# Who issues the stores of tiles that ScalarE makes last: SP or ScalarE

## The chip, the core and the metric

One core of a Trainium2 chip runs one program, the kernel. Its engines are TensorE (PE, with its weight loads as PEld), VectorE (DVE), ScalarE (ACT), GpSimd (POOL) and SyncE (SP). Each works through a queue of its own in order; they meet through semaphores. The metric is the device time of one execution in microseconds (us). In the profile, SPq and ACTq are the instruction queues of SP and ACT, in which DMAs are issued.

## The reference

One layer of a hybrid encoder, in float32, over 2048 tokens of width 1024:

```python
xn = rms_norm(x, mix_norm_g)
proj = xn @ w_in                  # aq ak av mq mk mv mo, two gate inputs, ga gm
att = chunk_band_attention(aq, ak, av, rel_bias)      # own chunk of 64 and 8 before
mqk = silu(causal_depthwise_conv(concat([mq, mk])))
hm = rms_norm(mlstm_chunkwise(mq_c, mk_c, mv, ipre + b_igate, fpre + b_fgate))
mlstm_out = sigmoid(mo) * hm
y = sigmoid(ga) * (att @ w_att_proj) + sigmoid(gm) * (mlstm_out @ w_mlstm_proj)
x = x + y @ w_out
hn = rms_norm(x, ffn_norm_g)
x = x + square(relu(hn @ w_up)) @ w_down              # hidden width 4096
out = rms_norm(x, final_norm_g)
```

## The kernel before

**Products.** A float32 product is made of three matmuls of fp32r parts (`mm3`, lines 644 to 646: a large and a small part on either side). The large weight matrices go through `quad` (line 727): a 2 by 2 block of weight tiles and of inputs is multiplied with seven products in place of eight, on sums and differences of the tiles; `quad_tok` (line 755) is the same for token tiles. A weight tile is loaded into `wraw` (lines 560, 565), split by ACT's cast (line 583) and DVE's difference (line 585) into the parts `wsp`, and sums of tiles are formed by DVE (line 602). PE takes `wsp` and the input parts `r`; the results come out of PSUM (`bank`) by ACT's copy (line 1859) and DVE's addition (line 1867) into `ctx` tiles.

**Stages.** The sequence is cut into two halves of two blocks each. In the trace, in us: up to 100 the norm and the first projections; 100 to 530 attention and recurrence of blocks 0 and 1, interleaved with projections; 530 to 700 the gates ga and gm of these blocks; 700 to 1100 the output product and the input products of blocks 2 and 3; 1100 to 1520 the up product of the first half; 1520 to 2070 its down product beside attention and recurrence of blocks 2 and 3; 2070 to 2250 the rest of that half's mixing; 2250 to 2500 the up product of the second half; then its down product and the final norm.

**Stores.** Tiles that don't fit into SBUF go to DRAM and are loaded again: kept projections `proj` (`keep_proj`, made by the copy of line 923), rows of norm scales (`row_out`, line 1125), values `mvfar` of the recurrence (`evac_mv`), gates `gate` and `mfar` (the finish of the gate and mo quads, lines 2000 and 2006), and the seven parts of the input to the down product, `u` (`keep` and `sums`; relu and square at lines 2198 and 2202, or sums on DVE). Every one of these goes through `store` (line 2120), which SP issues. All 2254 DMAs of the program are issued by SP.

**Order.** The program is written by generators; `Flow` runs them with priorities, pools of tiles and a clock for each engine. A yield such as `yield "sp", 900, 2000` tells it the engine, how long it is occupied and how much later the result is there. Then `Order` sorts the instructions of each engine anew by a list schedule: `cost` gives durations, `transfer`, `REACH` and `LAND` the time of a DMA over one shared queue, `due` the latest time, back from PE's sequence, `lag` the time of a signal, `MARGIN` the reserve behind an operation of another engine. The result is fixed as dependencies from each instruction to the next on its engine. The semaphores on which transfers report their landing aren't in this model: eight of them (DMAHW0 to DMAHW7 in the rows below) are given out in turn over the transfers of the program.

Of the kernel before, what the change touches and what calls it, by code (L numbers as in the profile page):

```python
# [30 lines left out]
P = 128  # L31
# [4 lines left out]
NT = T // P  # L36
# [33 lines left out]
class Event:  # L70
    def __init__(self):
        self.at = None
# [23 lines left out]
class Flow:  # L96
# [7 lines left out]
               act=dict(pe=220.0, act=130.0, dve=130.0, pool=180.0),  # L104
               dve=dict(pe=220.0, act=130.0, dve=130.0, pool=155.0), pool=dict(pe=290.0, act=130.0, dve=60.0),
               sp=dict())
# [106 lines left out]
def act_ns(n, ps=False, ap=0):  # L213
    return (51 if ps else 93) + 0.834 * n + 93 * ap
# [10 lines left out]
class Order:  # L225
# [6 lines left out]
    def __init__(self, tc):  # L232
        self.tc = tc
        name = lambda i: str(i.engine).split(".")[-1]
        self.ins = [i for i in tc.nc.cur_bb.bb.instructions if name(i) in self.WAKE and (i.ins or i.outs)]
        self.eng = [name(i) for i in self.ins]
        self.dur = [self.cost(i, e) for i, e in zip(self.ins, self.eng)]
        self.graph()

    @staticmethod  # L240
# [71 lines left out]

    def lag(self, j, k):
        e, to = self.eng[j], self.eng[k]
        if e == to != "SP":
            return 0.0
        t = self.WAKE[to] + (0.0 if e == "SP" else 13.0)
        return t + (0.0 if e != "PE" else 175.0 if self.dur[j] >= 140.0 else 130.0)

    def due(self):  # L320
        n, t = len(self.ins), 0.0
        due = [None] * n
        for k in range(n):
            if self.eng[k] == "PE":
                due[k] = t
                t += self.dur[k]
        for k in range(n - 1, -1, -1):
            d = t + 8000.0 if due[k] is None else due[k]
            less = self.dur[k] + (self.FAR if self.eng[k] == "SP" else 0.0)
            for j in self.succ[k]:  # L330
                d = min(d, due[j] - less - self.lag(k, j))
            due[k] = d
        return due

    def run(self):
        due, n = self.due(), len(self.ins)
        at, safe, left = [0.0] * n, [0.0] * n, self.left
        clock = dict.fromkeys(self.WAKE, 0.0)
        soon = {e: [] for e in self.WAKE}
        ripe = {e: [] for e in self.WAKE}  # L340
        order = {e: [] for e in self.WAKE}
        queue = 0.0
        for k in range(n):
            if not left[k]:
                heapq.heappush(soon[self.eng[k]], (0.0, due[k], k))
        for _ in range(n):
            t, e = min((clock[e] if ripe[e] else max(clock[e], soon[e][0][0]), e)
                       for e in self.WAKE if ripe[e] or soon[e])
            while soon[e] and soon[e][0][0] <= t:
                k = heapq.heappop(soon[e])[2]  # L350
                heapq.heappush(ripe[e], (k if e == "PE" else due[k], k))
            k = heapq.heappop(ripe[e])[1]
            order[e].append(self.ins[k])
            start = max(clock[e], at[k])
            clock[e] = end = start + self.dur[k]
            if e == "SP":
                queue = max(queue, start + self.REACH) + self.transfer(self.ins[k])
                end = queue + self.LAND
            for j in self.succ[k]:
                to = self.eng[j]  # L360
                r = end + self.lag(k, j)
                at[j] = max(at[j], r)
                safe[j] = max(safe[j], r + (self.MARGIN[e] if to != "PE" and (to != e or e == "SP") else 0.0))
                left[j] -= 1
                if not left[j]:
                    heapq.heappush(soon[to], (safe[j], due[j], j))
        for o in order.values():
            for a, b in zip(o, o[1:]):
                self.tc.add_manual_dep(b, a.name, mybir.DependencyInfo(
                    mybir.DependencyClass.NoSync, mybir.DependencyReason.DATA), reason="order")  # L370


class Layer:
# [215 lines left out]
    def quad_w(self, i, q, kept, raws, evs):  # L589
# [10 lines left out]
        def sub(n, dst, x, y):  # L600
            yield "dve", dve_ns(1024)
            V.tensor_sub(dst, x, y)  # L602
            if kept:
                fl.spawn(keep(n, dst), 1)
            else:
                fl.set(spilt[n])
# [312 lines left out]
    def keep_proj(self, x, j, bk):  # L919
        fl = self.fl  # L920
        (t,) = yield "get", self.temp, 1
        yield "act", act_ns(512, True)
        self.nc.scalar.copy(t[:, :512], bk)
        fl.put_dense(self.banks, bk)
        yield from self.store(self.projd.ap()[x, j], t[:, :512], self.proj_ev[x][j], self.temp, t)

    def merge_kept(self, j, t):

# [188 lines left out]
    def row_out(self, name, src):  # L1117

        fl, nc = self.fl, self.nc
        (t,) = yield "get", self.temp, 1  # L1120
        (bk,) = yield "get", self.banks, 1
        yield "pe", 220
        nc.tensor.transpose(bk[:NT, :P], src, self.ident)
        yield "act", act_ns(P, True)
        nc.scalar.copy(t[:NT, :P], bk[:NT, :P])
        fl.put(self.banks, bk)
        yield "sp", 900, 2000
        nc.sync.dma_start(self.rowd[name].ap().rearrange("(t p) -> t p", p=P), t[:NT, :P])
        fl.put(self.temp, t)

    def row_in(self, name, dst):
# [493 lines left out]
    def evac_mv(self, b, t, bk):  # L1625
        fl, nc = self.fl, self.nc
        (x,) = yield "get", self.ctx, 1
        yield "act", act_ns(512, True, 1 if b == 0 else 0)
        if b == 0:
            nc.scalar.mul(x[:, :512], bk, self.rr["x"][:, t:t + 1])  # L1630
        else:
            nc.scalar.copy(x[:, :512], bk)
        fl.put_dense(self.banks, bk)
        yield from self.store(self.mvfar[b].ap()[t], x[:, :512], self.mv_ev[b][t], self.ctx, x)

    def evac_conv(self, b, g, bk):
        fl = self.fl
# [263 lines left out]

    def keep(self, tiles, evs, k, dst, out):

        return self.sums(tiles, evs, lambda m, x: self.store(dst[m, k], x, out[m][k]), [e[k] for e in out])

    def sums(self, tiles, evs, go, sent):
        fl, V = self.fl, self.nc.vector
# [77 lines left out]
    def after_in(self, name, s):  # L1985
        fl, nc = self.fl, self.nc

        def finish(n, which, t, ps):
            hi, h = WHERE[which]
            b, j = 2 * s + h, 2 * hi + n  # L1990
            t5 = t[:, :512]
            if name in ("q", "k"):
                to, ev = (self.qfar, self.q_ev) if name == "q" else (self.kfar, self.k_ev)
                yield from self.parts(t, ps, 0.125 if name == "q" else 1.0, to[b].ap()[j], ev[b, j])
                return
            if name in ("mq", "mk"):
                yield from self.conv_far(b, (MH if name == "mk" else 0) + j, t, ps)
                return
            yield "act", act_ns(512)
            nc.scalar.activation(t5, t5 if ps is None else ps, AF.Tanh, scale=0.5)  # L2000
            if ps is not None:
                fl.put(self.banks, ps)
            if name == "mo":
                yield "act", act_ns(512, False, 2)
                g = self.ghead[:, j:j + 1]
                nc.scalar.activation(t5, t5, AF.Identity, scale=g, bias=g)
                dst, ev = self.mfar[b].ap()[2 * MH + j], self.m_ev[b, 2 * MH + j]
            else:
                x, j = name[:2] == "gm", 4 * hi + 2 * int(name[2]) + n
                if x and b == 0:  # L2010
                    yield from self.merge_kept(j, t)
                    return
                dst, ev = self.gd[b].ap()[int(x), j], self.g_ev[int(x), b, j]
            fl.spawn(self.store(dst, t5, ev, self.ctx, t), 1)

        return self.combine(finish, 3 if name in ("mq", "mk") else 0)

    def conv_far(self, b, g, z, ps):
# [99 lines left out]
    def store(self, dst, src, ev, pool=None, item=None):  # L2118
        yield "sp", 900, 2000
        self.nc.sync.dma_start(dst, src)  # L2120
        self.fl.set(ev)
        if pool is not None:
            self.fl.put(pool, item)
# [463 lines left out]
```

## Time and profile before

| | |
|---|---|
| median of 3 runs | 2779.6 us (2778.0 to 2780.48) |
| profiled execution | 2778.32 us, its span 2776.5 us |
| granted TensorE clock | 0.998 |
| busy: PE, DVE, ACT, POOL | 2751.0, 2057.1, 1494.5, 53.7 us |
| instructions: PE, DVE, ACT, POOL | 12994, 3783, 2608, 100 |
| DMA | 678.64 MB, 244 GB/s in the mean |

Busy time is the time in which an engine executes something; issuing a DMA does not count. A row of waits names the engine and line that stood still, the operation that ended its wait, and the total, the number and the longest of these waits in us. A row of a timeline gives start and duration in us, and in brackets the idle time before and what ended it. A row of DMA issues ends with the median us from issue to landing.

### The profile page before, as it was taken

How to read it: one execution, taken by the hardware profiler on the slowest of the kernel's cores; microseconds unless marked ns; L12 is line 12 of the kernel's file. 1: busy time of each engine (PE TensorE's matmuls, PEld its weight loads, DVE VectorE, ACT ScalarE, POOL GpSimd, SP SyncE). 2: the span in 40 equal slices, each digit the busy share in tenths (PEclk: the TensorE clock that was granted, in tenths of full speed). 3: DMA queues.
4: the chain of work that ended last, by engine and by line, in shares of the span. 5: the costliest groups of instructions: out<-in, count | busy, mean ns of one | idle time of the engine just before them, and what ended most of it. 6: DMA issues, size and time to landing. Idle time of an engine off the chain costs nothing.

```text
span 2776.5 us, 38600 instructions
## 1 busy us (share of the span) xinstructions
PE 2751.0 (99%) x12994; PEld 2286.5 (82%) x12994; DVE 2057.1 (74%) x3783; ACT 1494.5 (54%) x2608; POOL 53.7 (2%) x100
## 2 busy tenths in 40 slices
PE   9999999999999999999999999999999999999998
PEld 7888888888778878888888888888888888888887
DVE  7796789768996866886676688789888656556565
ACT  5564576535453535575555556565436655554443
POOL 0010001000000000000000000000000000000000
PEclk9999999999999999999999999999999999999999
DMA  7958759769755667579877887788777567666564
GB/s 273 291 195 276 230 166 304 250 222 319 262 199 204 220 243 256 198 270 325 288 280 273 287 245 233 230 256 253 251 261 261 206 220 261 243 238 217 189 230 149
DMA packets 329046, 678.64 MB, mean 244 GB/s; under 512 B 36840, under 2 KB 67728, under 8 KB 328848
## 3 DMA queue, kind: packets, MB, share of 16 engines
q1 hardware_dynamic: 328848, 676.18, 72.3%
q8 instruction: 102, 1.67, 0.2%
q14 instruction: 96, 0.79, 0.1%
HBM read 472.59 MB, written 203.44 MB: 243 GB/s over the span
## 4 chain that ended last, share of the span: by engine, by line
PE 91%; DMA 3%; DVE 3%; issue 2%; ACT 1%; SPq 0%; POOLq 0%; POOL 0%; DVEq 0%; ACTq 0%
PE bank L727 43%; PE bank L644 12%; PE bank L645 12%; PE bank L646 12%; PE bank L1415 2%; PE bank L1388 2%; PE bank L1446 2%; PE bank L755 2%; DVE wsp L585 1%; PE bank L1700 1%; PE bank L1701 1%; PE bank L1702 0%; PE bank L1686 0%; DMA wsum<-ctx 0%; ACT wsp L583 0%
## 5 line engine op out<-in xcount | busy, mean ns | idle before, releaser
L727 PE MATMUL bank<-r,wsp 128*128 128x512 f32 x5544 | 1265.5, 390 | 1.4 <-DVE ctx L1867 0.6
L727 PEld LDWEIGHTS bank<-r,wsp 128*128 128x128 f32 x5544 | 1038.0, 188 | 222.5 <-DVE ctx L1867 3.8
L585 DVE TENSOR_TENSOR wsp<-wraw,wsp 128x1024 fp32r<-128x1024 f32 x459 | 561.6, 1224 | 360.9 <-ACT wsp L583 335.2
L583 ACT CAST wsp<-wraw 128x1024 fp32r<-128x1024 f32 x459 | 482.5, 1052 | 464.1 <-PE bank L727 209.0
L644 PE MATMUL bank<-r,wsp 128*128 128x512 f32 x1472 | 586.1, 398 | 2.3 <-ACT r L1224 2.1
L645 PE MATMUL bank<-r,wsp 128*128 128x512 f32 x1472 | 574.8, 391 | 0.2 <-DVE r L1229 0.2
L646 PE MATMUL bank<-r,wsp 128*128 128x512 f32 x1472 | 574.9, 391 | 0.0
L646 PEld LDWEIGHTS bank<-r,wsp 128*128 128x128 f32 x1472 | 276.3, 188 | 58.7
L644 PEld LDWEIGHTS bank<-r,wsp 128*128 128x128 f32 x1472 | 276.9, 188 | 54.0 <-ACT r L1224 2.3
L645 PEld LDWEIGHTS bank<-r,wsp 128*128 128x128 f32 x1472 | 277.0, 188 | 50.5 <-DVE r L1229 0.5
L1867 DVE TENSOR_TENSOR ctx<-bank,ctx 128x512 f32<-128x512 f32 x186 | 127.1, 688 | 89.4 <-PE bank L727 89.2
L1229 DVE TENSOR_TENSOR r<-r 128x512 fp32r<-128x512 f32 x248 | 163.9, 687 | 25.3 <-ACT r L1224 24.5
L1224 ACT CAST r<-r 128x512 fp32r<-128x512 f32 x248 | 147.8, 624 | 49.8 <-DMA r<-u 47.0
L1859 ACT COPY ctx<-bank 128x512 f32<-128x512 f32 x186 | 107.9, 581 | 64.5 <-PE bank L727 60.9
L1430 ACT ACTIVATE sc<-sc,scs 128x640 f32<-128x640 f32 (+4 forms) x128 | 97.5, 763 | 71.7 <-DVE scs L1427 65.6
L2198 ACT ACTIVATE ctx<-ctx 128x512 f32<-128x512 f32 x96 | 60.6, 631 | 102.6 <-DVE ctx L1867 102.6
L1451 DVE TENSOR_TENSOR r<-bank,r 128x512 fp32r<-128x512 f32 (+1 forms) x168 | 97.1, 597 | 16.5 <-ACT r L1449 15.7
L1449 ACT CAST r<-bank 128x512 fp32r<-128x512 f32 (+1 forms) x168 | 81.8, 518 | 47.9 <-PE bank L1446 46.0
L1421 DVE CUSTOM_DVE_ANT_0 sc<-bank,bias 128x320 f32<-128x320 f32 (+3 forms) x240 | 103.7, 463 | 3.6 <-PE bank L1415 2.6
L1388 PE MATMUL bank<-r,r 128*128 128x512 f32 x336 | 96.0, 367 | 2.8 <-DVE r L1451 2.6
L602 DVE TENSOR_TENSOR wraw<-wraw,wraw 128x1024 f32<-128x1024 f32 x76 | 92.9, 1223 | 2.0
L552 DVE TENSOR_TENSOR ctx<-ctx,ctx 128x512 f32<-128x512 f32 x112 | 76.5, 688 | 17.7 <-DMA ctx<-in_wf 11.7
(258 smaller groups left out, 2720.7 us busy)
## 6 DMA issues: line engine op xcount, KB each, us to landing
wraw<-in_wf SPq DMA_DIRECT2D x178, 512.0 KB, 4.0
wraw<-wsum SPq DMA_DIRECT2D x136, 512.0 KB, 4.1
r<-u SPq DMA_DIRECT2D x224, 256.0 KB, 4.3
wraw<-in_w SPq DMA_DIRECT2D x88, 512.0 KB, 5.0
u<-ctx SPq DMA_DIRECT2D x128, 256.0 KB, 2.6
ctx<-in_wf SPq DMA_DIRECT2D x112, 256.0 KB, 4.3
wsum<-ctx SPq DMA_DIRECT2D x112, 256.0 KB, 3.6
u<-tmp SPq DMA_DIRECT2D x96, 256.0 KB, 3.7
```

The costliest lines, as they stand in the source:

```text
L583: nc.scalar.copy(w[:, 0], raw)
L585: nc.vector.tensor_sub(w[:, 1], raw, w[:, 0].bitcast(F32))
L644: mm(ps, lh, rh, start=first, stop=False)
L645: mm(ps, lh, rl, start=False, stop=False)
L646: mm(ps, ll, rh, start=False, stop=last)
L727: mm(ps, wv[:, x, k, n], a[:, y], start=new and k == 0 and x == y == 0, stop=k == 3 and x == 1, skip_group_check=True)
L1224: self.nc.scalar.copy(dst[:, 0], src)
L1229: self.nc.vector.tensor_sub(dst[:, 1], src, dst[:, 0].bitcast(F32))
L1388: nc.tensor.matmul(acc[:, :, c0:c0 + w], st, sl[:, :, o:o + w], start=n == 0, stop=n == total - 1)
L1421: nc.vector.tensor_tensor_reduce(out=e[:, x * w:x * w + w], in0=bks[x][:, :w], in1=br[:, j0 + x * w:j0 + x * w + w], op0=ALU.add, op1=ALU. ...
L1859: nc.scalar.copy(t[:, o:o + 512], ps)
L1867: nc.vector.tensor_add(t[:, o:o + 512], ps, t[:, o:o + 512])
```

## The change

`store_act` is a copy of `store` that issues on ScalarE (`nc.scalar.dma_start`). It is used for kept projections (16 stores), rows (10), `mvfar` of `evac_mv` (8), gates (56), `mfar` of the mo quads (8), and parts of `u` other than parts 2 to 5 (96 of 128 stores from `ctx`): 194 DMAs. In `Order`, rules that asked whether an instruction is on SP now ask whether it is a DMA, so that a DMA on ACT has the same duration (365 ns), the same shared queue and the same reserve.

```diff
+        self.dma = [type(i).__name__ == "InstDMACopy" or e == "SP" for i, e in zip(self.ins, self.eng)]
+        self.dur = [365.0 if d else self.cost(i, e) for i, e, d in zip(self.ins, self.eng, self.dma)]
...
-        if e == to != "SP":
+        if e == to and not self.dma[j] and not self.dma[k]:
             return 0.0
-        t = self.WAKE[to] + (0.0 if e == "SP" else 13.0)
+        t = self.WAKE[to] + (0.0 if self.dma[j] else 13.0)
...
-            if e == "SP":
+            if self.dma[k]:
                 queue = max(queue, start + self.REACH) + self.transfer(self.ins[k])
...
-        yield from self.store(self.projd.ap()[x, j], t[:, :512], self.proj_ev[x][j], self.temp, t)
+        yield from self.store_act(self.projd.ap()[x, j], t[:, :512], self.proj_ev[x][j], self.temp, t)
...
-        yield "sp", 900, 2000
-        nc.sync.dma_start(self.rowd[name].ap().rearrange("(t p) -> t p", p=P), t[:NT, :P])
+        yield "act", 420, 2000
+        nc.scalar.dma_start(self.rowd[name].ap().rearrange("(t p) -> t p", p=P), t[:NT, :P])
...
-        yield from self.store(self.mvfar[b].ap()[t], x[:, :512], self.mv_ev[b][t], self.ctx, x)
+        yield from self.store_act(self.mvfar[b].ap()[t], x[:, :512], self.mv_ev[b][t], self.ctx, x)
...
-        return self.sums(tiles, evs, lambda m, x: self.store(dst[m, k], x, out[m][k]), [e[k] for e in out])
+        return self.sums(tiles, evs, lambda m, x: self.store(dst[m, k], x, out[m][k]) if m in (2, 3, 4, 5) else
+                         self.store_act(dst[m, k], x, out[m][k]), [e[k] for e in out])
...
-            fl.spawn(self.store(dst, t5, ev, self.ctx, t), 1)
+            yield from self.store_act(dst, t5, ev, self.ctx, t)
...
+    def store_act(self, dst, src, ev, pool=None, item=None):
+
+        yield "act", 420, 2000
+        self.nc.scalar.dma_start(dst, src)
+        self.fl.set(ev)
+        if pool is not None:
+            self.fl.put(pool, item)
```

The changed kernel's lines 585, 1861, 2209 and 2213 are the lines 583, 1859, 2198 and 2202 of before; 2131 is the DMA of `store_act`. In brackets stand the semaphores on which an instruction waits.

ACT's queue in the up product, before, at about 1273 us of the trace: a copy out of PSUM, a weight cast, and relu and square of parts of `u`.

```order
L1859 COPY ctx_113<-bank_128 128x512 [waits PE_49]
L583 CAST wsp_63<-wraw_64 128x1024 [waits DMAHW4_49,PE_49]
L1859 COPY ctx_123<-bank_135 128x512 [waits DMAHW0_49,PE_49]
L2198 ACTIVATE ctx_113<-ctx_113 128x512 [waits DVE_49]
L2202 ACTIVATE ctx_113<-ctx_113 128x512 [waits Activation_49]
L583 CAST wsp_61<-wraw_67 128x1024 [waits DMAHW7_49,PE_49]
L2198 ACTIVATE ctx_123<-ctx_123 128x512 [waits DVE_49]
L2202 ACTIVATE ctx_123<-ctx_123 128x512 [waits Activation_49]
```

The same place now:

```order
L1861 COPY ctx_123<-bank_128 128x512 [waits DMAHW0_49,PE_49]
L585 CAST wsp_63<-wraw_64 128x1024 [waits DMAHW1_49,PE_49]
L1861 COPY ctx_122<-bank_132 128x512 [waits PE_49]
L2209 ACTIVATE ctx_123<-ctx_123 128x512 [waits DVE_49]
L2213 ACTIVATE ctx_123<-ctx_123 128x512 [waits Activation_49]
L2131 DMA u<-ctx_123 128x512 [waits DMAHW2_49,Activation_49]
L585 CAST wsp_61<-wraw_67 128x1024 [waits DMAHW1_49,PE_49]
L2209 ACTIVATE ctx_122<-ctx_122 128x512 [waits DVE_49]
L2213 ACTIVATE ctx_122<-ctx_122 128x512 [waits Activation_49]
L2131 DMA u<-ctx_122 128x512 [waits DMAHW3_49,Activation_49]
```

A store stands behind each square, the first of them ahead of a cast, and each waits for ACT itself and for a landing (DMAHW2, DMAHW3). Of the 194 stores, 164 carry such a wait for a landing.

SP's queue at the end of that up product, before, at about 1519 us: loads of attention's keys, queries and values (`kfar`, `qfar`, `vspill`), of down weights (`in_wf`), and stores of `u`.

```order
L1274 DMA r_91<-kfar 64x512 [waits DMAHW4_49]
L565 DMA wraw_67<-in_wf 128x1024 [waits DMAHW5_49,DVE_49]
L2120 DMA u<-ctx_127 128x512 [waits DMAHW6_49,Activation_49]
L1278 DMA r_74<-qfar 64x2x512 [waits DMAHW7_49,PE_49]
L1278 DMA r_74<-qfar 64x2x512 [waits DMAHW0_49]
L2120 DMA u<-ctx_123 128x512 [waits DMAHW1_49,Activation_49]
L1253 DMA r_77<-vspill 128x4x256 [waits DMAHW2_49,PE_49]
```

The same place now:

```order
L1276 DMA r_95<-kfar 64x512 [waits DMAHW7_49]
L567 DMA wraw_67<-in_wf 128x1024 [waits DMAHW0_49,DVE_49]
L1280 DMA r_74<-qfar 64x2x512 [waits DMAHW1_49,PE_49]
L1280 DMA r_74<-qfar 64x2x512 [waits DMAHW2_49]
L1255 DMA r_80<-vspill 128x4x256 [waits DMAHW3_49,PE_49]
```

The two stores are gone from between the loads; the landing semaphores, which go round in both, are now shared with the DMAs of ACT.

PE executes the same instructions; their order differs only within the stretches at about 50 to 500 and 1300 to 2000 us. The order on DVE, ACT and SP differs nearly everywhere up to about 2420 us, hardly at 950 to 1150, and not at all from about 2450 on.

More of the change, by code (lines that the diff above doesn't have):

```diff
@@ L236, in __init__ @@
         self.eng = [name(i) for i in self.ins]
-        self.dur = [self.cost(i, e) for i, e in zip(self.ins, self.eng)]
+        self.dma = [type(i).__name__ == "InstDMACopy" or e == "SP" for i, e in zip(self.ins, self.eng)]
+        self.dur = [365.0 if d else self.cost(i, e) for i, e, d in zip(self.ins, self.eng, self.dma)]
         self.graph()
@@ L328, in due @@
             d = t + 8000.0 if due[k] is None else due[k]
-            less = self.dur[k] + (self.FAR if self.eng[k] == "SP" else 0.0)
+            less = self.dur[k] + (self.FAR if self.dma[k] else 0.0)
             for j in self.succ[k]:
@@ L362, in run @@
                 at[j] = max(at[j], r)
-                safe[j] = max(safe[j], r + (self.MARGIN[e] if to != "PE" and (to != e or e == "SP") else 0.0))
+                far = "SP" if self.dma[k] else e
+                safe[j] = max(safe[j], r + (self.MARGIN[far] if to != "PE" and (to != e or self.dma[k]) else 0.0))
                 left[j] -= 1
```

## Prediction

> **What bounds the kernel now.** I read the page's head first (busy time by engine), then the busy time by stage, PE's waits, and then what SP and ACT wait for.
>
> ```profile
> span 2776.5 us, 38600 instructions
> PE 2751.0 (99%) x12994; PEld 2286.5 (82%) x12994; DVE 2057.1 (74%) x3783; ACT 1494.5 (54%) x2608; POOL 53.7 (2%) x100
> 542.97 114.64 PE bank L727 x504
> ```
>
> PE is busy for 2751.0 of 2776.5 us; 25.5 us remain. The third line, from the chain of waits, shows its pace: 504 matmuls in 114.64 us, one each 227 ns, with nothing between them. No matmul is added or removed, so only those 25.5 us can shrink. The stages (start:end, length, then busy time with the number of instructions of PE, PEld, DVE, ACT and POOL, then the clock granted, DMA share, GB/s):
>
> ```profile
> 0.00:100.00 100.00, 93.60 (x432) 75.53 (x433) 70.03 (x177) 53.07 (x91) 1.80 (x9) 1.00 0.84 285
> 100.00:530.00 430.00, 425.95 (x2254) 360.36 (x2253) 351.01 (x929) 266.22 (x612) 31.70 (x47) 1.00 0.75 242
> 530.00:700.00 170.00, 170.00 (x749) 139.97 (x748) 122.64 (x157) 73.70 (x106) 0.00 (x0) 1.00 0.74 260
> 700.00:1100.00 400.00, 396.24 (x1736) 321.74 (x1735) 306.12 (x428) 188.41 (x268) 0.00 (x0) 1.00 0.67 232
> 1100.00:1520.00 420.00, 420.00 (x1866) 346.28 (x1865) 311.10 (x426) 245.40 (x369) 0.58 (x4) 1.00 0.77 270
> 1520.00:2070.00 550.00, 547.66 (x2848) 464.92 (x2847) 455.62 (x1086) 300.08 (x630) 15.63 (x36) 1.00 0.80 255
> 2740.00:2777.00 37.00, 27.51 (x145) 22.96 (x143) 18.17 (x26) 12.17 (x18) 1.01 (x1) 0.93 0.39 142
> ```
>
> PE's gaps are 6.4 us in the first stage, 4.05 in 100 to 530 (the first attention stretch), 3.76 in 700 to 1100, 2.34 in 1520 to 2070 (the second), and 9.49 at the end. 530 to 700 (gates) and 1100 to 1520 (up product) have none. What ends the gaps, in PE's waits (total us, times, longest):
>
> ```profile
> PE bank L644 <- ACT r L1180: 6.4, 1, 6.4
> PE bank L1388 <- DVE r L1451: 2.6, 2, 2.1
> PE bank L755 <- DVE ctx L1867: 2.4, 2, 2.0
> PE bank L644 <- ACT r L1224: 2.1, 1, 2.1
> PE bank L1700 <- DMA r<-mvfar: 0.7, 1, 0.7
> PE bank L727 <- ACT r L1226: 0.2, 1, 0.2
> ```
>
> The 6.4 us are the start, before any store. The tail is the final norm, whose stores don't move. The L755 wait of 2.0 us lies in a stretch (950 to 1100) where the new program order of PE, DVE and ACT hardly differs, so I leave it. What the change can win at most is therefore 4.05 + 2.34 + (3.76 - 2.0) = 8.15 us: **the gain is capped near 8 us.** A loss has no such cap.
>
> **What the change takes off SP.** SP issues its DMAs in order, and stands still where a store's tile isn't made yet (waits of SP's queue):
>
> ```profile
> SPq L2120 <- ACT ctx L2202: 138.3, 80, 5.5
> SPq L2120 <- ACT ctx L2000: 65.6, 43, 4.4
> SPq L2120 <- ACT ctx L2006: 12.1, 8, 3.5
> SPq L2120 <- ACT tmp L923: 11.7, 10, 3.2
> SPq L2120 <- ACT tmp L1125: 11.5, 5, 3.4
> ```
>
> These 239.2 us go, since ACT issues the stores in its own order, behind the operation that makes the tile. It is worth something where a load, stuck behind such a wait, is late for PE. The one clear case is the chain at 1548 us (start, us, what):
>
> ```profile
> 1542.81 6.84 DMA r<-u
> 1549.67 0.63 ACT r L1224
> ```
> ```profile
> 1527.67 0.54 SPq L2120 DMA_DIRECT2D u<-ctx  x1
> 1542.81 2.02 SPq L2182 DMA_DIRECT2D r<-u  x4
> ```
>
> The load r<-u took 6.84 us from issue to use; PE then waited the 2.1 us of the L1224 row. Without the u<-ctx stores between the kfar and qfar loads SP may get there sooner. But SP there also stands at landings (rows further down), so I count half: -1.0. The two other removable waits (L1388, 2.6 us; L1700, 0.7 us) hang on attention chains in which no moved store is seen; -0.5 for both. Gain taken: **-1.5**, bounds 0 and -8.15.
>
> **What it puts on ACT: issue time.** 194 stores move. In the rows above a store takes SP 0.54 us, and 0.38 us in the shortest like it:
>
> ```profile
> 1519.85 0.38 SPq L2120 DMA_DIRECT2D u<-ctx  x1
> 1520.32 1.27 SPq L1278 DMA_DIRECT2D r<-qfar  x2
> ```
>
> 194 x 0.38 to 0.54 is 74 to 105 us on an engine with 2776.5 - 1494.5 = 1282 us idle. What hides it is this (ACT, then DVE, in the up product; in brackets the idle time before):
>
> ```profile
> 1276.38 0.63 ACT L2202 ACTIVATE ctx<-ctx 128x512 f32<-128x512 f32 x1
> 1277.49 1.06 ACT L583 CAST wsp<-wraw 128x1024 fp32r<-128x1024 f32 x1 [0.47 <-PE bank L727]
> 1279.83 2.49 DVE L602 TENSOR_TENSOR wraw<-wraw,wraw 128x1024 f32<-128x1024 f32 x2
> 1282.23 0.68 DVE L1867 TENSOR_TENSOR ctx<-bank,ctx 128x512 f32<-128x512 f32 x1
> ```
>
> Here the new order puts the store between L2202 and the cast L583; the cast waits 0.47 us for PE there, so 0 to 0.07 us of the issue shows. Behind it follow L585, both L602 and the addition L1867 on DVE, back to back, and PE takes that sum next. Eight quads have this pattern; at 0.13 us each they cost +1.0. Without the cover it is 8 x 0.54 = 4.3; if the issues of SP and ACT exclude each other, half of the 1.27 us row is added, 8 x 1.18 = 9.4. [...]
>
> **What it puts on ACT: landings of other transfers.** Each transfer reports its landing on one of eight semaphores, given out in turn over all of the program's transfers, and waits until the one eight places earlier has landed. That is seen on SP today, where a store is held by a load that it doesn't use (waits of SP from 950 to 985, and of the whole run):
>
> ```profile
> SPq L2120 <- DMA wraw<-in_wf: 2.2, 3, 0.9
> SPq L565 <- DMA wraw<-in_w: 4.6, 6, 0.9
> SPq L565 <- DVE wsp L585: 420.5, 185, 6.5
> ```
>
> On SP such a hold is short, at most 0.9 us, as the earlier transfer left the same queue long before. On ACT it need not be: 164 of the 194 stores have such a wait in the new order, most for a transfer that SP issues, and SP itself may stand up to 6.5 us (last row) before it issues that one. Queued behind the store on ACT are the casts L583 (and through them L585 and PE), the evacuations of banks, and the softmax.
>
> A transfer starts each 2776.5 / 2254 = 1.23 us, so eight places are 9.9 us, against a landing of 2.4 to 5.0 us (issue to landing, last column):
>
> ```profile
> wraw<-in_wf SPq DMA_DIRECT2D x178, 512.0 KB, 4.0
> wraw<-in_w SPq DMA_DIRECT2D x88, 512.0 KB, 5.0
> gate<-ctx SPq DMA_DIRECT2D x56, 256.0 KB, 2.4
> ```
>
> On average the wait is over already; it bites where SP bunches or is late. Laying the new order of transfers over the present times of issue gives an estimate of some 20 stores of the 194 that would meet it; at a landing of 5.0 us each that is 100 us of ACT held. How much of that comes through to PE? ACT's present stops for DMAs give a share:
>
> ```profile
> ACT r L1224 <- DMA r<-u: 47.0, 55, 5.9
> ACT r L1226 <- DMA r<-yp: 31.1, 13, 5.7
> ACT wsp L583 <- PE bank L727: 209.0, 147, 4.4
> ```
>
> The two make 78.1 us, of which PE waited 2.1 + 0.2: 3%. Those waits are foreseen by the planner, which orders around them; the holds by semaphores are not in its model, which knows transfers only by their data. The cast row shows the other cover: a weight cast is ahead of PE and waits for it 1.4 us in the mean, 4.4 at most, so a hold under 4 us mostly goes into that, while one of 6 to 11 doesn't. I take 8%, well above 3%: **+8.0**. Lower bound 3% of 60 us (12 stores), 1.8; upper bound 25% of 120 us (24 stores), 30.
>
> **The newly drawn order.** PE's order changes only in the attention stretches (about 50 to 500 and 1300 to 2000), DVE's, ACT's and SP's nearly up to 2420. The stretches have 4.05 + 2.34 us of gaps now. I take 0 for the redraw and +-6 for its range: it may remove all of them, or double them.
>
> **Sum.** -1.5 + 1.0 + 8.0 + 0 = +7.5. Profiled execution 2778.32 (span 2776.5, with 1.8 around it) + 7.5 = 2785.8; it lies 1.3 below the median of the runs, 2779.6, so about **2787**.
>
> **Rivals.** 0.2% (5.6 us) is about what a measurement of this kernel can tell from no change.
>
> - *No change* (0.33). The holds come through at 3%, 100 x 0.03 = 3.0, the issue costs 1.0 and 1.5 is won: +2.5, 2782. For it: the six PE rows come to 14.4 us although SP stood for 420.5 us at one line alone. Against it: this cover was planned. [...]
> - *Faster* (0.14). SP, rid of 239 us of standing, has loads ready earlier, and the gaps at 1548, in the attention stretches and at 717 to 860 go: at the cap 2779.6 - 8.1 = 2771.5. It needs at least 5.6 of 8.15 us, with no hold on ACT reaching PE: it decides that ACT's stores find their semaphore free. For it: eight places are 9.9 us. Against: more than two thirds of what is removable would have to vanish in one new order.
> - *Much slower* (0.12). A few ACT stores wait for a load that SP itself holds back until DVE frees a slot (the L565 row, 6.5), and for its landing (5.0): 11.5 us, of which 4.4 are covered. Four such stops, each passed on whole, give 28 us: 2807. It decides from about two of them on.
> - *The change doesn't do what it says* (0.01, within no change): the new order shows 194 DMAs on ACT's queue and as many fewer on SP's, so only the waits could stay.
>
> **How the numbers follow.** Forecast, slower by some 6 to 15 us: 0.41. No change: 0.33. Faster: 0.14. Much slower: 0.12. So faster 0.14, within 0.2% 0.33, slower 0.53. Low end: the capped gain, 2772. High end: +30 for the holds at their upper bound, +4.3 for uncovered issues, -1.5: +32.8, or 2812 (with the issues at 9.4, the holds may reach 25).
>
> **What would show it right or wrong.** Right: in the profile after, ACT's queue has waits of several us ended by DMAs that it doesn't read (wraw loads), casts L583 behind them start later, and PE has new waits on L583/L585 or on softmax chains in 100 to 530 and 1520 to 2070; the five L2120 rows on ACT products are gone. Wrong: ACT's queue shows hardly any wait for landings, or PE's busy time stays at 99% with gaps of 25 us or fewer; then the holds don't exist or are covered. If DVE or PE stages without moved stores (2500 to 2740) get longer, the whole reading fails.

## The result and the profile after

The changed kernel takes 2789.5 us in the median (2786.4 to 2792.1) where the kernel before has 2779.6: a ratio of 1.0031, interval [1.0018, 1.0044], 8.6 us (5.0 to 12.2) by that ratio; the two medians themselves lie 9.9 us apart. The profiled execution, at 2786.44 us, is the shortest of its five, 8.1 us above that of before. The head of its page:

```profile
span 2784.6 us, 38466 instructions
PE 2751.0 (99%) x12994; PEld 2285.4 (82%) x12994; DVE 2058.8 (74%) x3783; ACT 1497.7 (54%) x2608; POOL 48.8 (2%) x100
```

PE's busy time is the same to 0.1 us, so the 8.1 us of this execution are gaps. The four longer executions had a granted clock of 0.996 or 0.997, where this one and the profiled one of before had 0.998; 0.001 of 2780 us is 2.8 us, so part of their loss may be slower matmuls, which this profile does not show. By stage (columns as before):

```profile
0.00:100.00 100.00, 93.13 (x428) 75.08 (x429) 68.50 (x171) 52.33 (x90) 1.80 (x9) 1.00 0.84 280
100.00:530.00 430.00, 421.39 (x2235) 355.24 (x2234) 348.59 (x930) 265.78 (x611) 27.66 (x47) 1.00 0.77 243
530.00:700.00 170.00, 170.00 (x750) 140.16 (x749) 121.03 (x153) 74.49 (x106) 0.00 (x0) 1.00 0.74 254
700.00:1100.00 400.00, 397.44 (x1751) 323.68 (x1750) 310.16 (x433) 188.81 (x269) 0.00 (x0) 1.00 0.68 234
1100.00:1520.00 420.00, 420.00 (x1870) 345.95 (x1868) 312.69 (x428) 247.19 (x370) 0.58 (x4) 1.00 0.76 269
1520.00:2070.00 550.00, 543.36 (x2815) 460.72 (x2814) 450.50 (x1078) 299.64 (x628) 14.74 (x36) 0.99 0.81 254
```

The gaps grew in the two attention stretches: 4.05 to 8.61 us at 100 to 530, and 2.34 to 6.64 us at 1520 to 2070; elsewhere they changed by at most 1.2 us. The gate stage and the up product of the first half, which are full of moved stores, still have none. PE's waits name the places:

```profile
PE bank L646 <- ACT r L1226: 5.7, 2, 5.0
PE bank L1688 <- DMA r<-mfar: 3.0, 1, 3.0
PE bank L1448 <- DVE sc L1436: 2.3, 1, 2.3
PE bank L757 <- DVE ctx L1869: 1.8, 2, 1.4
```

The 5.0 us are the old stall at 1548 us, which had 2.1, now at 1551; the 3.0 us are new, at 453 us. The chain at 1551 us (start, us, what), and those waits of SP between 1490 and 1545 us that a landing of u ended:

```profile
1547.38 0.23 PE bank L648
1547.64 7.96 DMA r<-u
1555.62 0.63 ACT r L1226
1556.29 2.08 PE bank L646 x4
```
```profile
SPq L599 <- DMA u<-ctx: 3.9, 1, 3.9
SPq L1276 <- DMA u<-ctx: 3.4, 2, 3.1
SPq L1280 <- DMA u<-ctx: 0.4, 1, 0.4
```

SP issues the load of u on which the chain hangs at 1547.64, where it was 1542.81. Shortly before, it stood 7.7 us for landings of stores of u, at line 599 (a store of a weight sum) and lines 1276 and 1280 (loads of keys and queries), none of which reads u. In the kernel before the same kind of wait comes to 0.3 us in this window. So the semaphores do couple the queues, but in the other direction from the one that I priced: **SP waits for ScalarE's stores, not ScalarE for SP's loads.**

Laying the program's turn of semaphores on the landing times of the trace gives the same for the whole run (a reckoning, not a row): SP was held by landings of ScalarE's stores 18 times, 33.4 us, at most 3.9; ScalarE by SP's transfers 3 times, 1.4 us, and by its own once, 1.2 us. SP's total is a rough one: some of its instructions waited for an engine as well, and as these are counted it comes to 16 to 21 holds and 22 to 38 us. The issue on ScalarE is short (instruction, count, shortest/median/longest ns):

```profile
L2131 ACTq DMA_DIRECT2D u<-ctx x96: 326/327/383, 1230.3 to 2460.8; - x96
L2131 ACTq DMA_DIRECT2D gate<-ctx x56: 326/326/676, 519.7 to 1176.9; - x56
```

### The profile page after: what moved, and what is told of

Read it like the earlier page. It is cut to its first block, busy times and chain, and to the rows that moved or that the text cites. A ratio compares the mean times of both kernels' runs of the same rounds, so it can differ in the third digit from the quotient of the medians.

```text
span 2784.6 us, 38466 instructions
## 1 busy us (share of the span) xinstructions
PE 2751.0 (99%) x12994; PEld 2285.4 (82%) x12994; DVE 2058.8 (74%) x3783; ACT 1497.7 (54%) x2608; POOL 48.8 (2%) x100
## 4 chain that ended last, share of the span: by engine, by line
PE 91%; DMA 3%; DVE 3%; issue 2%; ACT 0%; SPq 0%; POOL 0%; POOLq 0%; DVEq 0%; ACTq 0%
PE bank L729 44%; PE bank L646 12%; PE bank L647 12%; PE bank L648 12%; PE bank L1417 2%; PE bank L1390 2%; PE bank L1448 2%; PE bank L757 1%; DMA r<-u 1%; DVE wsp L587 1%; DVE ctx L2041 0%; DMA wraw<-in_wf 0%; DMA wsum<-ctx 0%; DMA ctx<-in_xt 0%; PE bank L1688 0%
## 5 line engine op out<-in xcount | busy, mean ns | idle before, releaser
L554 DVE TENSOR_TENSOR ctx<-ctx,ctx 128x512 f32<-128x512 f32 x112 | 76.6, 687 | 14.8 <-DMA wsum<-ctx 9.8
```

## The experiments

The theories: **A**, landings of ScalarE's stores hold SP through the shared semaphores; **B**, the newly drawn order of the attention stretches costs by itself; and that of the prediction, ScalarE held by SP's landings. The change alters two things at once, who issues and what order the planner draws. The first two kernels separate them.

### Who issues, and in which order

The planner gets a virtual engine for the moved stores, and each is put into its real queue at its planned start; the rows of PE, DVE and GpSimd are then those of one kernel, with the issuer of the other.

```diff
+        self.real = [name(i) for i in self.ins]
+        self.eng = ["SP" if type(i).__name__ == "InstDMACopy" else e for i, e in zip(self.ins, self.real)]
...
+            begun[self.real[k]].append((start, len(begun[self.real[k]]), self.ins[k]))
...
+        order = {e: [x[2] for x in sorted(o, key=lambda x: x[:2])] for e, o in begun.items()}
```

Old order, ScalarE issues the 194:

> ScalarE issues the 194 stores, but every other engine keeps the order of the kernel before (the planner still counts these stores to SP, and each is put into ScalarE's queue at its planned start). Theory A, landing semaphores: transfers of the two queues hold each other's issue, here as in the changed kernel, so most of the loss of 9 us is here too: 2785 to 2790 us, with SP waiting for landings of gate, u, mvfar or proj stores (18 such holds, 33 us, in the changed kernel). Theory B, the newly drawn order: the loss came with the order of the attention stretches alone, so this is 2777 to 2782 us. Theory of the prediction, ScalarE held: 2784 to 2790 us, with ScalarE waiting for landings.

Measured: 1.0026 [1.0017, 1.0035]. New order, SP issues (the same edit, with the 194 counted to ScalarE by the planner):

> SP issues all stores again, but every engine has the order of the changed kernel, the 194 stores put into SP's queue at their planned start. Theory A, landing semaphores: the loss goes, 2777 to 2782 us. Theory B, the newly drawn order: it stays, 2786 to 2792 us, with PE's stalls at about 453 us (3.0 us) and 1551 us (5.0 us) in place.

Measured: 1.0024 [1.0016, 1.0033]. Its stalls at 452 and 1552 us are there, at 2.2 and 3.5 us:

```profile
PE bank L652 <- ACT r L1233: 3.5, 1, 3.5
PE bank L1695 <- DMA r<-mfar: 2.2, 1, 2.2
```

So the order alone costs 6.7 us with no store moved, and the issuer alone cost 7.2 us here (a second measurement of that kernel, further down, has 2.5); neither theory alone holds, and the two do not add up to the 8.6 us of the change. In both kernels the 194 stores stand in a queue that they weren't planned for, which may cost something by itself. To see what any new order costs, the kernel before was drawn anew with another reckoning of a store on SP:

```diff
     def store(self, dst, src, ev, pool=None, item=None):
-        yield "sp", 900, 2000
+        yield "sp", 860, 2000
```

> The kernel before, with 860 in place of 900 ns as the program writer's reckoning of a store on SP: no store moves, but the order of the attention stretches is drawn anew, as much as by the change. Theory B: a time that differs from before by several us, in either direction, with other stalls of PE at 450 and 1550 us. Theory A: within 2 us of 2779.6.

> The same with 940 ns, a second draw. Theory B: several us off 2779.6, and not by the same stalls as with 860. Theory A: within 2 us of 2779.6.

Measured: 1.0034 [1.0022, 1.0046] with 860, 1.0007 [0.9999, 1.0016] with 940. With the order of the change, three new draws cost 9.4, 2.0 and 6.7 us with SP as the issuer. **The order of before is better than two of the three**; the draw with 940 can't be told from it, and its time alone fits theory A as well as B. The draw of the change lies between the other two. Both have waits of PE on r<-mfar that before lacks, as the change has (860, then 940):

```profile
PE bank L1675 <- DMA r<-mfar: 4.3, 2, 2.8
```
```profile
PE bank L1686 <- DMA r<-mfar: 2.5, 1, 2.5
```

### Who issues, in the old order

Only the engine of the 194 stores is changed, in the kernel of the first experiment:

```diff
+    def moved(self, name):
+        n, Layer.n_moved = Layer.n_moved, Layer.n_moved + 1
+        return self.nc.gpsimd
...
-        self.nc.scalar.dma_start(dst, src)
+        self.moved(dst.tensor.name).dma_start(dst, src)
```

(the other kernels return `self.nc.scalar if name == "u" else self.nc.sync`, the reverse of it, `self.nc.sync if n in (11, 47, 50, 94, 97, 104, 116, 135, 137, 139) else self.nc.scalar`, and `self.nc.gpsimd if name == "u" else self.nc.scalar`).

> As the old order with ScalarE issuing, but GpSimd issues the 194 stores: its transfers report on eight semaphores of their own, so SP isn't held by their landings, nor they by SP's. Theory A, shared landing semaphores: the 7 us of the first experiment go, 2776 to 2780 us where before has 2777.8. Rival, that freeing SP of the stores is harmful in itself (transfers bunch, loads land later): 2783 to 2788 us, with the stall near 1551 us as long as there.

> Old order, ScalarE issues only the 96 stores of u. Theory A: SP is held at about 1504 and 1520 us by landings of u, PE's stall near 1551 us is longer by 1.5 to 4 us, that at 450 to 470 us is as before: plus 2 to 5 us. Rival, that the loss comes from the attention of blocks 0 and 1: no difference from before.

> Old order, ScalarE issues the other 98 stores (gates, mfar, kept projections, mvfar, rows), SP those of u. Theory A: SP is held by landings of proj near 468 us, PE's stalls between 450 and 470 us grow by 2 to 4 us, that at 1551 us is as before: plus 2 to 5 us in all. Rival, that only the stores of u cost: no difference.

> As the first experiment, but the 10 stores of the 194 whose landing held SP by more than 0.1 us there (1 proj, 2 gates, 7 u) are issued by SP again; the turn of the semaphores stays. Theory A: about two thirds of the 7 us go, plus 0 to 3 us. Rival, that ScalarE's issue itself or the other 184 stores cost: still plus 6 to 8 us.

> Old order, GpSimd issues the 96 stores of u on semaphores of its own, ScalarE the other 98. Landing semaphores: no hold of SP at the end of the up product, so as with u on SP, 0.998 to 1.0005 of before. Rival, that a third issuing engine adds transfers in flight and makes loads land later there: 1.001 to 1.003, with the stall at 1546 us above 3 us.

> The first experiment once more, beside the others, with a second profile. If its two halves (u, and the rest) add up, the time is within 2 us of before, and the 7 us of the first time were the chip's or the executions'; if not, 1.0018 to 1.0035 again. The profile shows whether the step of 5 us at 462 to 475 us, which the half with proj on ScalarE did not have, belongs to the kernel: it is there again, or only the step at 1546 us is (4 to 6 us).

The table has the ratio, SP's waits for landings of u between 1490 and 1545 us (sum of such rows), PE's longest wait between 1535 and 1575 us, and how much further behind the same matmul of before PE is at 1580 than at 1540 us (from the starts of each matmul in the two profiles).

| u issued by, others by | ratio | SP for u | PE's wait | step |
|---|---|---|---|---|
| SP, SP (before) | 1 | 0.3 | 2.1 | 0 |
| GpSimd, GpSimd | 1.0003 [0.9994, 1.0011] | 0 | 2.7 | +1.7 |
| GpSimd, ScalarE | 1.0003 [0.9994, 1.0012] | 0 | 1.4 | +1.0 |
| SP, ScalarE | 0.9991 [0.9982, 1.0000] | 0.5 | 0.7 | -1.3 |
| ScalarE, SP | 1.0001 [0.9992, 1.0010] | 6.6 | 4.6 | +4.4 |
| ScalarE, both | 1.0026 [1.0017, 1.0035] | 8.6 | 3.7 | +3.9 |
| ScalarE, both, again | 1.0009 [1.0001, 1.0018] | 7.5 | 3.8 | +4.0 |
| ScalarE but for 10 | 1.0015 [1.0006, 1.0024] | 9.0 | 6.6 | +6.3 |

Where u is issued by ScalarE, SP waits 6.6 to 9.0 us for its landings and PE falls back by 3.9 to 6.3 us at this one stall; where another engine issues u, it is -1.3 to 1.7. The step is not the wait alone: around its end the clock was 0.50 for 6.8 us with u alone on ScalarE, 0.50 for 3.4 us with u on GpSimd and the rest on ScalarE, and 1.00 in the kernel before (rows in the last section). In both runs of the old order with all 194 on ScalarE, too, matmuls behind the wait took 0.43 us each; with u on SP and the rest on ScalarE they followed each other in 0.23 us. One such hold in the second run of the old order (SP's timeline, then ScalarE's):

```profile
1492.82 0.45 SPq L2193 DMA_DIRECT2D r<-u  x1
1497.24 0.32 SPq L600 DMA_DIRECT2D wsum<-wraw  x1
```
```profile
1490.95 0.63 ACT L2213 ACTIVATE ctx<-ctx 128x512 f32<-128x512 f32 x1
1491.62 0.33 ACTq L2131 DMA_DIRECT2D u<-ctx  x1
```
```profile
SPq L600 <- DMA u<-ctx: 4.0, 1, 4.0
SPq L1277 <- DMA u<-ctx: 3.3, 1, 3.3
```

ScalarE issues a store as soon as its square is done, at 1491.62. SP is free at 1493.27, but line 600 is eight places behind that store in the turn, and stands until it has landed, at 1497.24. With SP as the issuer (the kernel before) the wait is for the product alone, 0.2 us ahead of the store at 1493.72, and the landing passes while SP issues seven others: its waits for landings of u come to 0.3 us up to 1545.

GpSimd is the control: in the built program its transfers report on eight semaphores of their own (DMASW0 to DMASW7). SP's waits for u are then gone, PE's wait is 1.4 and 2.7 us, and the step shrinks to 1.0 and 1.7 us, although SP is as free of the stores as with ScalarE; in the run with 1.0 the half clock (0.50 for 3.4 us) makes up 1.7 us by estimate, more than the step. So it is the shared turn, not the freeing of SP, that costs. One rival is left: GpSimd differs from ScalarE in more than its semaphores (its issue took 0.54 us, against 0.33), and ScalarE with semaphores of its own was not tried.

Taking 10 stores back was expected to save two thirds of the loss. It didn't: with them on SP the turn fell on other stores, and two new holds of 5.5 and 3.5 us came in the same 30 us:

```profile
SPq L1622 <- DMA u<-ctx: 5.5, 1, 5.5
SPq L1282 <- DMA u<-ctx: 3.5, 1, 3.5
```

Two things in the table don't fit. The halves were expected at +2 to +5 us each and came out at +0.3 and -2.5, although the step at 1546 us is in the first of them as expected: PE was 1.9 us ahead of before when it came there. Most of this lead is clock: the profiled execution of before ran at 0.50 of the clock for 3.4 us from 122.8 and again from 976.1, each behind a wait of PE of about 2 us; the half with u lacks the second of these stretches, and the other half, 4.6 us ahead at its end, lacks both. The hold of SP at 466 us that the second half has (5.5 us, for the landing of a proj store) reached PE nowhere. And the same program gave 7.2 us in one session and 2.5 in another, on another chip, with a step of 5 us at 462 to 475 us in the first profile only: a wait of 3.0 us for r<-mfar, and behind it a matmul of 128x512 at 0.43 us, where 0.23 is usual. Of the other profiles with all or most proj stores on ScalarE, two have a shorter wait there (1.7 us with u on GpSimd, 1.1 with the ten on SP) and two have none; those with proj on SP or GpSimd have none either. So that step is not shown to be the kernel's; a ratio of one session carries a spread of a few us beyond its interval, and the steps within the profiles are the firmer evidence.

### Who issues, in the two other draws

> The order of the 860 ns draw (with SP issuing it was at 1.0034 of before), ScalarE issues the 194 stores. Landing semaphores: SP is held by u's landings at the end of the up product, and the time is 2 to 7 us above that draw with SP: ratio 1.004 to 1.006. Order alone: as with SP, 1.0025 to 1.0045.

> The order of the 940 ns draw (with SP issuing 1.0007 of before), ScalarE issues the 194 stores. Landing semaphores: PE's stall at 1545 to 1570 us grows by 2 to 6 us, ratio 1.0015 to 1.003. Order alone: 0.9997 to 1.0015.

The edit is that of the first experiment, with 860 and 940 in `store` and `store_act`. Measured: 1.0045 [1.0031, 1.0058] and 1.0021 [1.0012, 1.0030]. Both lie where theory A had them; the first is also the upper end of what the order alone would give. With the two orders above that makes four pairs, each member against before in its own session:

| order | SP issues | ScalarE issues | SP's waits for u, both | step at 1540 to 1580 |
|---|---|---|---|---|
| before | 1 | 1.0026 and 1.0009 | 0.3, 8.6 and 7.5 | +3.9 and +4.0 |
| 860 | 1.0034 | 1.0045 | 0.5, 10.8 | +2.8 |
| 940 | 1.0007 | 1.0021 | 0.9, 14.8 | +5.4 |
| the change | 1.0024 | 1.0031 | 2.0, 7.7 | +1.0 |

ScalarE is the slower issuer in all four, by 2 to 4 us (7 in one session), though with 860 and with the order of the change the difference is smaller than the intervals. The step at the end of the up product is in all four, smallest where the order had a stall of 3.5 us there already. In the 940 draw, SP's three largest and PE's:

```profile
SPq L600 <- DMA u<-ctx: 5.1, 1, 5.1
SPq L1621 <- DMA u<-ctx: 5.0, 1, 5.0
SPq L1277 <- DMA u<-ctx: 4.4, 2, 3.5
```
```profile
PE bank L1418 <- DVE tmp L1400: 5.5, 1, 5.5
```

With SP as issuer that draw's longest wait there is 1.6 us. By the pair of the change, its 8.6 us are 6.7 us of order and 2 us of issuer. Each has an interval of 2 to 4 us on either side: that the order costs is clear of it, that the issuer costs here rests on the other pairs and on the step.

No version beats both kernels beyond doubt: u on SP and the rest on ScalarE, in the old order, is at 0.9991 with an interval that ends at 1.0000, and its profile owes most of its lead to the clock.

## Why the prediction came out right

The number and the sign are right, but by luck and not for the reason given. By the prediction's own sign its mechanism is wrong: ScalarE's queue shows hardly any wait for landings, and PE's two longest waits in the changed stretches, 5.0 and 3.0 us, hang on late loads (r<-u, r<-mfar), not on casts behind a held ScalarE. By its steps:

- **The cap on the gain and PE as the bound** held: PE's busy time is 2751.0 us before and after, and no version gained more than 2.5 us.
- **SP freed, -1.5**: the five rows of SP waiting for ScalarE's products are gone from SP's queue, as forecast, but nothing came of it. At 1548 us the loads left later, not earlier: between 1490 and 1545 us SP had waited only 0.2 us for products of line 2202 in the kernel before, and now waited 7.7 us for landings of u.
- **Issue on ScalarE, +1.0**: 0.33 us each and no gap in the stages where the tight quads lie: 0. Two inputs of this term were off. The 0.13 us per quad follows from no row; the rows beside it give 0 to 0.07 us, 0.6 in all. And 0.38 to 0.54 us for a store was read off the few rows shown, while the whole of them on SP, before, has a median of 0.32 (shortest/median/longest ns):

```profile
L2120 SPq DMA_DIRECT2D u<-ctx x128: 319/320/1297, 1227.0 to 2460.4; - x128
```

  The bound of 9.4 us, for issues that exclude each other, isn't borne out either: if that were common, ScalarE's issues would spread beyond 0.33 us, while their median is at the shortest; one store of proj took 1.17 us. No run here shows an exclusion of issues as a cost.
- **ScalarE held by landings, +8.0**: this is the step that failed. I took 20 stores at 5.0 us; it was 4 stores and 2.6 us. A store stands behind a product of ScalarE, and by then the transfers of eight places earlier had landed in all but these cases. That such a hold of SP was at most 0.9 us before was read off two rows; a third row of the whole run has 1.5 (`SPq L1278 <- DMA r<-vspill: 3.3, 3, 1.5`). The mistake was to look in one direction: the turn of the semaphores binds both ways, and here the queue that ran ahead, SP's, waited for the one that ran behind: 18 times, against 3 times the other way. Measured in its place: some 33 us of holds on SP, of which 2 to 4 us came through by the pairs above.
- **The newly drawn order, 0 with +-6**: mis-sized. Three draws cost 2.0, 6.7 and 9.4 us. The stretches' few gaps could have been the sign that this order was a good one out of many, so that a new draw is likelier to lose than to win; three draws support this and no more.
- **The rivals.** *No change* came out with GpSimd as the issuer, at 1.0003, where SP had no wait for landings of u; no row of before could bear on another issuer, since SP alone issued. With ScalarE the rival, like the forecast, counted holds of ScalarE and missed those of SP. The rival *much slower* had SP's loads hold ScalarE; ScalarE's longest hold was 1.2 us.

Two errors of opposite direction, +8.0 for a hold that was 2.6 us and 0 for an order that was 6.7, brought the sum to the measured place. That is luck.

## What to carry to other kernels

In this program the transfers of two queues take landing semaphores in one turn, and moving stores to the second queue tied the two together. In a like case ask for both directions which queue runs ahead, since here that one was held some 33 us by the landings of the other, and the other 1.4 us by its. A change that makes a scheduler draw a new order must be split from it before it is judged: keep the order and change the issuer, keep the issuer and change the order, and draw the old one a few times with neutral numbers. In this schedule, with nearly no gaps, two of three redraws cost several us by themselves (6.7 and 9.4), as much as the effect that is looked for. And before a few us between two profiles are read as the kernel's, ask the granted clock in narrow windows behind each longer wait of PE.

## What was not expected of the hardware

The longer stall of PE cost more than its length. Behind a wait of 4.57 us (u on ScalarE, old order), matmuls of 128x512 followed each other in about 0.43 us for 4.7 us, and in 0.23 us again from 1555.9; behind the 2.06 us of before, in 0.23 us by 1552.1 (u on ScalarE, then before).

```profile
1550.93 0.80 PE L648 MATMUL bank<-r,wsp 128*128 128x512 f32 x1 [4.57 <-ACT r L1228]
1553.53 0.63 PE L649 MATMUL bank<-r,wsp 128*128 128x512 f32 x1
1553.96 0.63 PE L648 MATMUL bank<-r,wsp 128*128 128x512 f32 x1
1555.93 0.39 PE L650 MATMUL bank<-r,wsp 128*128 128x512 f32 x1
1556.16 0.39 PE L649 MATMUL bank<-r,wsp 128*128 128x512 f32 x1
```
```profile
1550.34 0.49 PE L644 MATMUL bank<-r,wsp 128*128 128x512 f32 x1 [2.06 <-ACT r L1224]
1552.10 0.39 PE L645 MATMUL bank<-r,wsp 128*128 128x512 f32 x1
1552.33 0.40 PE L644 MATMUL bank<-r,wsp 128*128 128x512 f32 x1
```

That is about 2 us on top, and explains the step of +4.4 us where the wait grew by 2.5. The granted clock shows it when the window is narrow; the mean of the whole stretch (0.99) hardly does. The rows are in the columns of the stages; the eighth, before the DMA share, is the clock (first u on ScalarE, then u on GpSimd and the rest on ScalarE, then before, all in the old order):

```profile
1548.90:1555.70 6.80, 4.77 (x12) 3.45 (x13) 4.54 (x7) 3.13 (x5) 0.00 (x0) 0.50 1.04 396
1550.90:1554.30 3.40, 3.40 (x11) 2.63 (x10) 3.40 (x5) 1.38 (x3) 0.00 (x0) 0.50 1.03 395
1550.40:1554.00 3.60, 3.37 (x15) 2.54 (x16) 3.34 (x5) 2.40 (x4) 0.00 (x0) 1.00 1.05 401
```

PE is busy for 4.77 us of the first window, and at half the clock that is 2.4 us lost, by estimate. The same windows at the two earlier stalls (before twice, then u on ScalarE, then the rest on ScalarE twice):

```profile
122.80:126.10 3.30, 3.30 (x12) 3.01 (x13) 2.95 (x16) 0.99 (x4) 0.29 (x2) 0.50 1.06 251
976.10:979.50 3.40, 3.40 (x10) 2.62 (x9) 3.37 (x5) 0.00 (x0) 0.00 (x0) 0.50 1.04 411
```
```profile
974.70:979.00 4.30, 4.26 (x19) 3.55 (x20) 4.05 (x5) 0.00 (x0) 0.00 (x0) 1.00 1.05 413
```
```profile
122.80:130.00 7.20, 7.20 (x37) 6.12 (x38) 6.81 (x27) 5.29 (x13) 0.29 (x2) 1.00 1.02 300
973.00:981.00 8.00, 7.85 (x35) 6.53 (x36) 6.71 (x10) 2.81 (x5) 0.00 (x0) 1.00 1.05 409
```

The stretches at half the clock are 3.4 or 6.8 us long in these rows. The half clock came behind a wait of 4.57 us (u on ScalarE), of 1.4 us (u on GpSimd, the rest on ScalarE) and of 2.0 us (before, at 976), and did not come behind 2.1 us (before, at 1550) or 2.3 us (the rest on ScalarE, at 973). The length of a wait doesn't decide alone, and what does is open. The prediction had left this out: part of the difference between two profiles of the same order is which waits met it.

GpSimd's issue of these stores took 0.54 us, against 0.33 on ScalarE, with no loss that could be measured:

```profile
L2136 POOL DMA_DIRECT2D u<-ctx x96: 542/542/597, 1225.2 to 2453.9; - x96
```
